# Turning tables by one DMA per tile in a one-core transformer block: the residual blocks join, one SwiGLU tile leaves

## The chip, the core and the metric

The kernel runs on one core of one Trainium2 chip. The metric is the device time of one execution in microseconds (us), as the median of several runs. Times of engines and of single instructions come from the hardware profiler's record of one execution. Engine names are those of the profile: PE is the matmul engine (PEld its weight loads), DVE the vector engine, ACT the scalar engine, POOL is GpSimd, and SP the engine whose queue starts nearly all transfers.

## The reference, cut to what matters

A block over 256 tokens (two tiles of 128) with a model width of 2048, in float32:

```python
h = rmsnorm(x, g_mix); proj = h @ w_in                     # two gated token mixers follow
x = x + (sigmoid(g_sb) * (y_sb @ w_sb_out) + sigmoid(g_ca) * (y_ca @ w_ca_out)) @ w_mix_out
h = rmsnorm(x, g_ffn)
g_ff, u_ff = split(h @ w_ffn_in, 2)                        # D_FF = 5632 each
x = x + (silu(g_ff) * u_ff) @ w_ffn_out
h = rmsnorm(x, g_ple)
x = x + sigmoid(h @ w_ple_gate) * (p @ w_ple_in)           # the "ple" gate, the last matrix
out = rmsnorm(x, g_final)
```

The weights are read from HBM once each and are most of the traffic (284 MB read in all).

## The kernel before

**Products.** Every matmul is split for float32 accuracy: the weights into a rounded part `hi` and a rest `lo` (ACT casts `hi`, DVE subtracts for `lo`), the activations likewise, and three products are added (hi·hi, hi·lo, lo·hi). The activations are the stationary operand. They lie transposed in *tables* (`T[:, kt, 0 or 1, token]`, part 0 the rounded one, part 1 the rest), where `kt` numbers the 128 rows of the inner dimension. Three tables matter here: `T3` (the residual for the FFN's input matmuls, 16 rows kt in 4 blocks of 512 columns of x), `T2` (the SwiGLU's result, one tile of 512 columns at a time), and `T1` (the residual for the last gate, "ple"). The names `T_5123`, `T_71` and `T_72` of the listings below are the places of T3, T1 and T2.

**Pieces.** The weights go by in *pieces* of two kt. A plain piece is 12 matmuls of 128x512. A *pair* piece takes two pieces' weights at once with sums and differences of them (a Strassen-like form, own accumulators `su`): 21 matmuls. Its weights pass through more casts: `L298` and `L301` for the two `hi`, `L304` for the sums (`T<-xf`). Pair pieces need sums of the table's blocks too, made by `sums_of` (tiles `fm`, then `FP`, `F_more` or `F_last`).

**Order.** A list `pieces` and the function `flush` set the order: for each piece it starts loads on SP's queue as one of seven places for raw weights comes free (`RAW` and `MORE` in this part of the program), splits up to three pieces ahead, issues the piece's products, and then runs whatever *asides* are due at that piece's number (`state["at"]`) and one of the waiting `tasks` (`later(fn)` puts a task back by three). Each engine works through its own instructions in the order in which the program issued them; semaphores join them. So an instruction that is issued early and waits holds everything behind it on its engine.

**The FFN** runs in three blocks of the hidden width, h0, h1 and h2, with 3, 4 and 4 SwiGLU tiles of 512 columns. Each block's input units are followed by out units that multiply the tiles with `w_ffn_out`. The FFN's first unit has no pair pieces: its 16 plain pieces (here p0 to p15) run through `T3` as it is, and in the meantime `scale_next` multiplies the table by the norm's factor (`L869`) and `pair_sums` makes the sums (`L890`, then `fm`), using the two work places called `af`.

**Two ways to turn a tile** stand in the kernel. `into_table` lets PE transpose 128x128 blocks into PSUM (8 per tile, `tp`), and `table_part` copies from there into the table: with a gain by ACT (`L556`) and DVE (`L557`). The residual blocks (four for `T3`, four for `T1`) and the mixers' gates go that way. `into_table_by_dma` splits the 32-bit words into 16-bit halves with two ACT copies (`L502`), transposes by two DMAs on SP's queue (`L505`, 128x8x128 each), and later joins the halves with two ACT copies for each half of the tile (`L513`), into a work place `af`, from which `table_part` fills the table (`L548` for a pair block). All 11 SwiGLU tiles go that way: the DMAs two pieces after the tile is made, the joins four and five pieces later.

Of the kernel before, what the change touches and what calls it, by code (L numbers as in the profile page):

```python
# [9 lines left out]
F32 = mybir.dt.float32  # L10
F32R = mybir.dt.float32r
U16 = mybir.dt.uint16
# [5 lines left out]
P = 128  # L18
S = 256
NT = 2  # L20
# [12 lines left out]
NB = 512  # L33
FB = 256
FF_BLOCKS = [12, 16, 16]

PAIRS = (2, 4, 6)
# [16 lines left out]
def block_kernel(ctx: ExitStack, tc: tile.TileContext, x, p, w_in, w_sb_out, w_ca_out, w_mix_out,  # L54
# [18 lines left out]
    nc = tc.nc  # L73
    dma_w = nc.sync
# [25 lines left out]
    x_ = bp.tile([P, NT, D], F32, tag="x", name="x")  # L100
# [52 lines left out]
    asides = []  # L153
    turning = set()
    done = set()
# [251 lines left out]
    state = dict(loaded=0, split=0, at=0, raw=0, hl=0, ext=0, ps=ps_mm, fourth=None, ring=0, places=0, hold=False)  # L407
    late = dict(ps=[ps_mm])
# [27 lines left out]
    def later(fn, n=3):  # L436

        for _ in range(n):
            tasks.append((None, lambda: None))
        tasks.append((None, fn))  # L440
# [53 lines left out]
        for k in range(4):  # L494
            done.add((key, 4 * c + k))

    def turn(src, planes, whole):

        words = src.bitcast(U16).rearrange("p t (n h) -> p t h n", h=2)
        planes = planes.bitcast(U16).rearrange("p t (h n) -> p t h n", h=2)  # L500
        for t in range(NT):
            nc.scalar.copy(planes[:, t], words[:, t])  # L502
        for t in range(NT):
            ts = slice(t * P, (t + 1) * P)
            dma_w.dma_start_transpose(whole[:, :, ts], planes[:, t].rearrange("p h n -> p (h n)"))  # L505

    def turned_part(dst, kt, turned, k0, gain, key, forms, pairs):

        af = state["work"]("af").rearrange("p (k s) -> p k s", k=2)
        words = af.bitcast(U16).rearrange("p k (s h) -> p h k s", h=2)  # L510
        with tc.issue_after(state["cast"].ins):
            for h in range(2):
                nc.scalar.copy(words[:, h], turned[h][:, k0 : k0 + 2, :])  # L513
        table_part(dst, kt + k0, af, gain, forms, pairs, af)
        for k in range(k0, k0 + 2):
            done.add((key, kt + k))

    def into_table_by_dma(dst, c, src, planes, rooms, key, gain=None, forms=None, pairs=PAIRS, wait=2):

        turned, whole = rooms  # L520
        turning.update((key, 4 * c + k) for k in range(4))
        at = state["at"] + wait
        steps = [(at, lambda: turn(src, planes, whole))]
        for i in range(2):
            steps.append((at + 4 + i, lambda i=i: turned_part(dst, 4 * c, turned, 2 * i, gain, key, forms, pairs)))
        asides.extend(steps)
        asides.sort(key=lambda v: v[0])

    def room_halves(v):

        v = v.rearrange("p t n -> p (t n)").bitcast(U16)
        return [u.rearrange("p (k s) -> p k s", s=S) for u in (v[:, :1024], v[:, 1024:])], v.rearrange("p (k s) -> p k s", s=S)

    def table_part(dst, kt, ps, gain, forms, pairs, af=None):
        n = ps.shape[1]
# [398 lines left out]
    room = bp.tile([P, 4096], F32R, tag="x", name="room")  # L934
# [81 lines left out]

    def next_tables(T, c, gain, key, pool):

        for cc in (c - 1, c):
            fn = lambda cc=cc: into_table(T, cc, x_[:, :, cc * NB : (cc + 1) * NB], gain, key, pool=pool)  # L1020
            if cc == c:
                tasks.append((None, fn))
            else:
                later(fn)
# [67 lines left out]
    def out_form(pairs):  # L1092
        return lambda kt: late["F"][1][pairs.index(kt // 2)]

    def hidden(dst, c, key, g, pairs):
        C = late["C"]
        into_table_by_dma(dst, c, C[:, :2, :], C[:, 2:, :], room_halves(C[:, :2, :]), key, forms=out_form(pairs), pairs=pairs)

    def in_post(dst, c, key, pairs):
        def post(g, b):  # L1100
# [37 lines left out]
    k0 = 0  # L1138
# [131 lines left out]
```

## Time and profile before

| | us |
|---|---|
| median of 3 runs | 1458.44 (1457.09 to 1458.54) |
| the profiled execution | 1458.38 |
| its span, first to last instruction | 1456.7 |
| PE busy in it | 1438.7 (99%) |
| DVE busy | 1248.6 (86%) |
| ACT busy | 869.8 (60%) |

The mean granted TensorE clock of that execution is 0.996 of full speed. Busy times are of one execution on the one core; a busy PE isn't a PE at its peak, since matmuls overlap each other by their pipeline. A row of a group reads: line, engine, operation, output and input with their sizes, count, then busy time, the mean of one in ns, and after the bar the idle time of the engine just before such instructions and what ended it. A row of the timeline reads: start, length, engine, line, operation, count, and in brackets the idle time before and what ended it.

### The profile page before, as it was taken

Reading aid. Unit: us, or ns where it says so; the run is one execution under the profiler, and the core shown is the slowest. Engines: PE = TensorE matmul, PEld = TensorE weight load, DVE = VectorE, ACT = ScalarE, POOL = GpSimd, SP = SyncE. Lnnn points to the kernel's source line nnn. Section 1 sums busy time; section 2 is a strip of 40 time slices with the busy share of each in tenths; the row PEclk is TensorE's granted clock in tenths of the full one; section 3 lists DMA queues with packets and bytes.
Section 4 is the critical chain, followed back from the end, with each engine's and each line's share of the span. In section 5 each row is a group of like instructions: output and inputs, shape, how many; then the busy total and the mean of one; then the engine's idle time right before and its main releaser. Section 6 shows DMA issues by size and latency. Waiting matters only on the chain.

```text
span 1456.7 us, 18609 instructions
## 1 busy us (share of the span) xinstructions
PE 1438.7 (99%) x6749; PEld 1200.4 (82%) x6749; DVE 1248.6 (86%) x1587; ACT 869.8 (60%) x1048; POOL 24.1 (2%) x44
## 2 busy tenths in 40 slices
PE   9999999999999999999999899999999999999997
PEld 7888888878888888888888688888888888887886
DVE  6879777888987767888989899999999999999775
ACT  6445555654545665555767555667755666776652
POOL 0200000000010000000000000000000000000000
PEclk9999999999999999999999999999999999999999
DMA  9866555566675556765675666776666766675771
GB/s 315 285 188 210 181 173 173 177 202 200 201 253 166 180 164 183 232 203 174 204 218 187 183 212 194 223 226 210 198 205 221 218 203 213 222 211 179 262 231 70
DMA packets 187964, 296.95 MB, mean 204 GB/s; under 512 B 32256, under 2 KB 65328, under 8 KB 187616
## 3 DMA queue, kind: packets, MB, share of 16 engines
q1 hardware_dynamic: 185760, 287.09, 63.6%
q0 software_dynamic: 2112, 8.68, 1.8%
q8 instruction: 53, 0.87, 0.3%
q14 instruction: 39, 0.32, 0.1%
HBM read 284.19 MB, written 5.77 MB: 199 GB/s over the span
## 4 chain that ended last, share of the span: by engine, by line
PE 89%; DVE 4%; DMA 3%; ACT 2%; issue 1%; SPq 0%; DVEq 0%; ACTq 0%
PE mm L313 63%; PE su L313 11%; PE mm L398 8%; PE mm L400 4%; DVE lo L260 2%; DMA C<-C 1%; DVE xf L260 1%; DMA raw<-in_w_ffn_out 1%; DMA raw<-in_w_ple_in 1%; PE tp L490 1%; ACT hi L283 1%; DMA raw<-in_w_ffn_in 0%; PE mml L313 0%; ACT af L513 0%; DVE raw L260 0%
## 5 line engine op out<-in xcount | busy, mean ns | idle before, releaser
L313 PE MATMUL mm<-hi,T 128*128 128x512 f32 x2650 | 855.1, 391 | 1.6 <-DVE v L902 1.0
L260 DVE TENSOR_TENSOR lo<-raw,hi 128x1024 fp32r<-128x1024 f32 (+1 forms) x517 | 624.4, 1217 | 114.0 <-ACT hi L283 100.8
L283 ACT CAST hi<-raw 128x1024 fp32r<-128x1024 f32 (+1 forms) x379 | 395.9, 1049 | 329.0 <-PE mm L313 205.8
L313 PEld LDWEIGHTS mm<-hi,T 128*128 128x128 f32 x2650 | 497.3, 188 | 106.4 <-issue 1.4
L313 PE MATMUL mm<-lo,T 128*128 128x512 f32 x1325 | 516.1, 390 | 0.0
L313 PEld LDWEIGHTS mm<-lo,T 128*128 128x128 f32 x1325 | 248.9, 188 | 51.0
L398 PE MATMUL mm<-T,hi 128*128 128x512 f32 x512 | 179.7, 398 | 0.0
L400 PE MATMUL mm<-T,lo 128*128 128x256 f32 x512 | 139.5, 280 | 0.0
L301 ACT CAST hi<-raw 128x1024 fp32r<-128x1024 f32 x69 | 72.6, 1052 | 77.3 <-DVE raw L260 28.0
L260 DVE TENSOR_TENSOR T<-xf,T 128x1536 fp32r<-128x1536 f32 x61 | 106.9, 1753 | 12.6 <-ACT T L304 12.5
L398 PEld LDWEIGHTS mm<-T,hi 128*128 128x128 f32 x512 | 94.5, 188 | 20.1
L260 DVE TENSOR_TENSOR xf<-raw 128x512 f32<-128x512 f32 x138 | 94.5, 685 | 13.8 <-DMA raw<-in_w_ffn_out 5.2
L304 ACT CAST T<-xf 128x1536 fp32r<-128x1536 f32 x61 | 90.3, 1480 | 20.3 <-DVE xf L260 19.7
L400 PEld LDWEIGHTS mm<-T,lo 128*128 128x128 f32 x512 | 96.5, 189 | 2.3
L298 ACT CAST hi<-raw 128x1024 fp32r<-128x1024 f32 x69 | 72.5, 1051 | 36.7 <-PE mm L313 21.8
L313 PE MATMUL mm<-T,T 128*128 128x512 f32 (+1 forms) x279 | 77.8, 373 | 0.0
L313 PE MATMUL su<-hi,T 128*128 128x512 f32 x170 | 66.3, 392 | 5.1 <-ACT T L548 5.1
L313 PEld LDWEIGHTS mm<-T,T 128*128 128x128 f32 x279 | 49.5, 189 | 9.2
L902 DVE TENSOR_TENSOR C<-su,C 128x512 f32<-128x512 f32 x72 | 47.6, 682 | 0.7 <-PE su L313 0.5
L260 DVE TENSOR_TENSOR xf<-raw,xf 128x512 f32<-128x512 f32 x69 | 47.2, 684 | 0.6
L260 DVE TENSOR_TENSOR raw<-raw 128x512 f32<-128x512 f32 x69 | 47.2, 684 | 0.3
L313 PE MATMUL su<-T,FP 128*128 128x512 f32 x174 | 47.2, 389 | 0.0
(280 smaller groups left out, 1266.0 us busy)
## 6 DMA issues: line engine op xcount, KB each, us to landing
raw<-in_w_ffn_in SPq DMA_DIRECT2D x176, 512.0 KB, 4.3
raw<-in_w_in SPq DMA_DIRECT2D x160, 512.0 KB, 4.3
raw<-in_w_ffn_out SPq DMA_DIRECT2D x88, 512.0 KB, 4.7
raw<-in_w_mix_out SPq DMA_DIRECT2D x32, 512.0 KB, 4.7
raw<-in_w_ple_gate SPq DMA_DIRECT2D x32, 512.0 KB, 5.1
raw<-in_w_sb_out SPq DMA_DIRECT2D x16, 512.0 KB, 3.8
raw<-in_w_ca_out SPq DMA_DIRECT2D x16, 512.0 KB, 4.5
x<-in_x SPq DMA_DIRECT2D x4, 512.0 KB, 10.6
```

Of the source, the lines that this page charges most:

```text
L260: return nc.vector.tensor_tensor(out, a, b, ALU.subtract)
L283: state["cast"] = nc.scalar.copy(hi[:, c : c + m], raw[:, c : c + m])
L298: nc.scalar.copy(h1, raw1)
L301: nc.scalar.copy(h2, raw2)
L304: nc.scalar.copy(xh, xf)
L313: state["mm"] = nc.tensor.matmul(ps, u, v, start=first, stop=last, skip_group_check=True)
L398: nc.tensor.matmul(ps, hi[:, i, f], lhs[:, kt, :, :].rearrange("p c s -> p (c s)"), start=a, stop=False)
L400: nc.tensor.matmul(ps[:, :S], lo[:, i, f], lhs[:, kt, 0, :], start=False, stop=z)
L490: nc.tensor.transpose(ps[:, k, t * P : (t + 1) * P], src[:, t, (k0 + k) * P : (k0 + k + 1) * P], ident)
L902: nc.vector.tensor_tensor(C[i], q, C[j], ALU.add)
```

## The change

- `by_dma` takes the place of `turn`, `turned_part`, `into_table_by_dma` and `room_halves`. It issues one DMA transpose of 128x16x128 per tile, not two of 128x8x128, and one join copy of 128x2x512 for each half of a tile, not two of 128x512. The caller gives the piece numbers of the DMA and of the first join.
- The last SwiGLU tile of h0 (`c == 2`) goes back to PE: 8 transposes through `later(into_table)`.
- `next_tables`: the four residual blocks for `T3` and the first two for `T1` ("ple") go by DMA. The first block of a unit is split into `C[:, :2]` and turned into an own place `turned` (DMA one piece later, joins five and six later); the second is split into `C[:, 2:]` and turned into `C[:, :2]`, that is into the place which the first DMA reads (three, seven and eight pieces later). The ple blocks 2 and 3 stay on PE.

So PE transposes of tables and gates go from 96 to 56 (8 for the h0 tile are new, 48 for six residual blocks are gone), and DMA transposes from 22 small to 16 large ones.

```diff
-    def turn(src, planes, whole):
...
-    def turned_part(dst, kt, turned, k0, gain, key, forms, pairs):
...
-    def into_table_by_dma(dst, c, src, planes, rooms, key, gain=None, forms=None, pairs=PAIRS, wait=2):
...
+    def by_dma(dst, c, src, planes, turned, key, at, gain=None, forms=None, pairs=PAIRS):
+
+        words = src.bitcast(U16).rearrange("p t (k n h) -> p t h k n", h=2, n=P)
+        planes, turned = (v.rearrange("p t n -> p (t n)").bitcast(U16) for v in (planes, turned))
+        split = planes.rearrange("p (h k t n) -> p t h k n", h=2, k=4, t=NT)
+        halves = turned.rearrange("p (h k s) -> p h k s", h=2, k=4)
+
+        def turn():
+            for t in range(NT):
+                nc.scalar.copy(split[:, t], words[:, t])
+            dma_w.dma_start_transpose(turned.rearrange("p (j s) -> p j s", s=P), planes)
+
+        def join(k0):
+            af = state["work"]("af").rearrange("p (k s) -> p k s", k=2)
+            with tc.issue_after(state["cast"].ins):
+                nc.scalar.copy(af.bitcast(U16).rearrange("p k (s h) -> p h k s", h=2), halves[:, :, k0 : k0 + 2, :])
+            table_part(dst, 4 * c + k0, af, gain, forms, pairs, af)
+            for k in range(k0, k0 + 2):
+                done.add((key, 4 * c + k))
+
         turning.update((key, 4 * c + k) for k in range(4))
+        asides.extend([(state["at"] + at[0], turn), *((state["at"] + at[1] + i, lambda i=i: join(2 * i)) for i in range(2))])
         asides.sort(key=lambda v: v[0])
...
     def next_tables(T, c, gain, key, pool):
+        C = late["C"]
+        room = late["pool"].tile([P, 2, NB], F32, tag="turned", name="turned")
         for cc in (c - 1, c):
+            if key == "ffn" or cc < 2:
+                planes, turned, at = (C[:, :2, :], room, (1, 5)) if cc < c else (C[:, 2:, :], C[:, :2, :], (3, 7))
+                by_dma(T, cc, x_[:, :, cc * NB : (cc + 1) * NB], planes, turned, key, at, gain)
+                continue
...
     def hidden(dst, c, key, g, pairs):
         C = late["C"]
-        into_table_by_dma(dst, c, C[:, :2, :], C[:, 2:, :], room_halves(C[:, :2, :]), key, forms=out_form(pairs), pairs=pairs)
+        if key == "h0" and c == FF_BLOCKS[0] // 4 - 1:
+            later(lambda: into_table(dst, c, C[:, :2, :], key=key, pool=g["pool"], forms=out_form(pairs), pairs=pairs))
+        else:
+            by_dma(dst, c, C[:, :2, :], C[:, 2:, :], C[:, :2, :], key, (2, 6), forms=out_form(pairs), pairs=pairs)
```

What this does to the order of work is seen on two engines and one queue. In the changed kernel the lines below `by_dma` have other numbers: `L506` is the split copy (`L502` before), `L507` the DMA (`L505`), `L512` the join (`L513`), `L543` and `L544` the table's parts with a gain (`L556`, `L557`), `L856` the scaling of the table (`L869`), `L877` the pair sums' copy (`L890`).

**ACT in the FFN's first unit,** in the engine's order (an `xN` sums up equal neighbours), from the norm's sums (`jk,sum_ffn`) to the pair sums' first cast (`FP<-fm`). Before:

```order
L283 CAST hi<-raw 128x1024
L125 ACTIVATE jk,sum_ffn<-x 128x512 x2
L283 CAST hi<-raw 128x1024 x2
L556 ACTIVATE T_5123<-tp,gT 128x256 x4
L283 CAST hi<-raw 128x1024
L556 ACTIVATE T_5123<-tp,gT 128x256 x4
L283 CAST hi<-raw 128x1024 x6
L478 CAST FP<-fm 128x512
L283 CAST hi<-raw 128x1024 x3
```

With the change, from the table's block 2 (kt 8 to 11) to the second `FP`:

```order
L543 ACTIVATE T_5123<-af,gT 128x256 x2
L283 CAST hi<-raw 128x1024
L543 ACTIVATE T_5123<-af,gT 128x256 x2
L283 CAST hi<-raw 128x1024 x6
L478 CAST FP<-fm 128x512
L512 COPY af<-C 128x2x512
L283 CAST hi<-raw 128x1024
L543 ACTIVATE T_5123<-af,gT 128x256 x2
L512 COPY af<-C 128x2x512
L543 ACTIVATE T_5123<-af,gT 128x256 x2
L304 CAST T_71<-xf 128x1536
L478 CAST FP<-fm 128x512
```

Before, both blocks' parts (two times four `L556`) stood ahead of the six casts and of `FP`. With the change block 3 (kt 12 to 15) is joined only behind the first `FP`, and its first `L543` stands behind one cast more, that of p15, which waits for p11's matmuls, since it takes the place of p11's `hi`.

**ACT in the last out unit of h2,** where ple blocks 0 and 1 are turned. Its second half runs plain and pair pieces in the order 0,0,1,-2,1,-4,3,-5,3,-6,7,7 (a minus is a pair piece). Before, from the sums of pair -2 (`L304`) to `L301` of pair -5:

```order
L304 CAST T_5123<-xf 128x1536
L556 ACTIVATE T_71<-tp,gT 128x256
L125 ACTIVATE jk,sum_ple<-x 128x512 x2
L556 ACTIVATE T_71<-tp,gT 128x256
L298 CAST hi<-raw 128x1024
L556 ACTIVATE T_71<-tp,gT 128x256 x4
L283 CAST hi<-raw 128x1024
L556 ACTIVATE T_71<-tp,gT 128x256 x2
L301 CAST hi<-raw 128x1024
L298 CAST hi<-raw 128x1024
L304 CAST T_5123<-xf 128x1536
L283 CAST hi<-raw 128x1024
```

With the change, from the joins of block 0 to that same `L301` of pair -5, the last row:

```order
L512 COPY af<-turned 128x2x512 x2
L301 CAST hi<-raw 128x1024
L304 CAST T_5123<-xf 128x1536
L298 CAST hi<-raw 128x1024
L543 ACTIVATE T_71<-af,gT 128x256 x4
L283 CAST hi<-raw 128x1024
L512 COPY af<-C 128x2x512
L543 ACTIVATE T_71<-af,gT 128x256 x2
L512 COPY af<-C 128x2x512
L543 ACTIVATE T_71<-af,gT 128x256 x2
L301 CAST hi<-raw 128x1024
```

The eight table parts stood ahead of pair -4's `L301` before. Between `L304` of pair -4 and `L301` of pair -5 there was one cast; now there are two casts, two joins and all eight table parts.

**SP's queue** (transfers, summed up where they repeat). Before, around the FFN's start and at h0's last tile:

```order
L244 DMA raw<-in_w_mix_out 128x2x512 x32
L244 DMA raw<-in_w_ffn_in 128x2x512 x26
L505 DMA_TRANSPOSE C<-C 128x8x128 x2
L244 DMA raw<-in_w_ffn_in 128x2x512 x19
L505 DMA_TRANSPOSE C<-C 128x8x128 x2
L244 DMA raw<-in_w_ffn_in 128x2x512 x3
L244 DMA raw<-in_w_ffn_out 128x2x512 x14
L505 DMA_TRANSPOSE C<-C 128x8x128 x2
```

With the change:

```order
L244 DMA raw<-in_w_mix_out 128x2x512 x27
L507 DMA_TRANSPOSE turned<-C 128x16x128
L244 DMA raw<-in_w_mix_out 128x2x512 x2
L507 DMA_TRANSPOSE C<-C 128x16x128
L244 DMA raw<-in_w_mix_out 128x2x512 x3
L244 DMA raw<-in_w_ffn_in 128x2x512 x11
L507 DMA_TRANSPOSE turned<-C 128x16x128
L244 DMA raw<-in_w_ffn_in 128x2x512 x2
L507 DMA_TRANSPOSE C<-C 128x16x128
```

Four transposes now stand among the loads for the mixers' last matrix and the FFN's first; the second of each two waits for the first one's landing, with the loads behind it. The pair for h0's last tile is gone.

More of the change, by code (lines that the diff above doesn't have):

```diff
@@ L495, in into_table @@
             done.add((key, 4 * c + k))
-    def turn(src, planes, whole):
[L499 to L505, printed above, removed]
-    def turned_part(dst, kt, turned, k0, gain, key, forms, pairs):
[L509 to L516, printed above, removed]
@@ L518, in into_table_by_dma @@
-    def into_table_by_dma(dst, c, src, planes, rooms, key, gain=None, forms=None, pairs=PAIRS, wait=2):
-        turned, whole = rooms
-        turning.update((key, 4 * c + k) for k in range(4))
[L522 to L526, printed above, removed]
+    def by_dma(dst, c, src, planes, turned, key, at, gain=None, forms=None, pairs=PAIRS):
[14 more added lines that the diff above has]
+                done.add((key, 4 * c + k))
+        turning.update((key, 4 * c + k) for k in range(4))
+        asides.extend([(state["at"] + at[0], turn), *((state["at"] + at[1] + i, lambda i=i: join(2 * i)) for i in range(2))])
@@ L527, in into_table_by_dma @@
         asides.sort(key=lambda v: v[0])
-    def room_halves(v):
-        v = v.rearrange("p t n -> p (t n)").bitcast(U16)
-        return [u.rearrange("p (k s) -> p k s", s=S) for u in (v[:, :1024], v[:, 1024:])], v.rearrange("p (k s) -> p k s", s=S)
     def table_part(dst, kt, ps, gain, forms, pairs, af=None):
```

## Prediction

> **What bounds the kernel now.** I read the page's busy times first, then its chain and PE's waits, and then the timeline around the longest wait.
>
> ```profile
> PE 1438.7 (99%) x6749; PEld 1200.4 (82%) x6749; DVE 1248.6 (86%) x1587; ACT 869.8 (60%) x1048; POOL 24.1 (2%) x44
> PE 89%; DVE 4%; DMA 3%; ACT 2%; issue 1%; SPq 0%; DVEq 0%; ACTq 0%
> PE su L313 <- ACT T L548: 5.1, 1, 5.1
> PE warm L628 <- POOL mhalf L109: 1.2, 1, 1.2
> ```
>
> PE sets the time: 99% busy and 89% of the chain. So only three things count: matmul work taken from or given to PE, stalls of PE, and its clock. Of its waits one stands out, 5.1 us in a single place; the next is 1.2. The profiled execution (1458.38) agrees with the median of the runs (1458.44), so the sum can stand on either.
>
> The long wait belongs to h0's last tile. First the chain that ends there, then PE and SP, then PE in three windows (length, busy with count, granted clock, DMA share, GB/s):
>
> ```profile
> 801.35 0.81 SPq L505
> 802.22 7.47 DMA C<-C
> 809.77 1.38 ACT af L513 x2
> 812.39 0.62 ACT T L548
> ...
> 806.23 0.62 PE L313 MATMUL mm<-hi,T 128*128 128x512 f32 x2
> ...
> 806.91 0.62 PE L313 MATMUL mm<-hi,T 128*128 128x512 f32 x2
> ...
> 807.59 0.39 PE L313 MATMUL mm<-hi,T 128*128 128x512 f32 x1
> 813.05 0.79 PE L313 MATMUL su<-hi,T 128*128 128x512 f32 x1 [5.08 <-ACT T L548]
> 800.80 5.51 SPq L505 DMA_TRANSPOSE C<-C  x2
> 797.00:807.50 10.50, 10.50 (x48) 1.00 0.94 178
> 813.00:819.00 6.00, 5.95 (x14) 0.50 0.50 165
> 819.00:830.00 11.00, 11.00 (x49) 1.00 0.33 98
> ```
>
> Two DMA transposes take 7.47 us to land while the 16 DMA engines are 94% taken; then come the joins (`L513`), the table (`L548`), and only then a matmul. And the six microseconds that follow run at half clock.
>
> **The change part by part.** *h0's tile back to PE: the stall.* Three matmuls take 806.91 − 806.23 = 0.68, a pitch of 0.2267 each, so a plain piece of twelve is 2.72. From 807.59 to 813.05 are 5.46 us, so 5.2 are lost. With PE's own transposes there is no transfer and no join. −5.2. What comes next behind it is the copy of the transposes out of PSUM, some tenths; the later pieces' casts were done by 805.79 + 1.05 already, so nothing else is waiting there.
>
> *The clock after it.* 14 matmuls took 6.0 us; at the full pitch they take 3.2. −2.8, as long as no new stall is long enough to do the same.
>
> *PE transposes.* The residual blocks' transposes, as they stand among matmuls (timeline), with their group and the table parts that go with them:
>
> ```profile
> 669.53 0.40 PE L313 MATMUL mm<-hi,T 128*128 128x512 f32 x1
> 669.76 1.04 PE L490 MATMUL tp<-ident,x 128*128 128x128 f32 x8
> 670.56 0.48 PE L313 MATMUL mm<-hi,T 128*128 128x512 f32 x1
> L490 PE MATMUL tp<-ident,x 128*128 128x128 f32 x64 | 8.5, 272 | 0.0
> L556 ACT ACTIVATE T<-tp,gT 128x256 fp32r<-128x256 f32 x32 | 13.6, 473 | 3.5 <-DVE T L557 3.0 <-PE tp L490 0.5
> ```
>
> From 669.76 to 670.56 eight transposes hold PE for 0.80 us, and in none of the 64 did PE wait (idle 0.0). Six tiles gone: −4.8. One tile (h0's) back: +0.8. The Trainium skill's page "VectorE: DVE Perf Modes", section "Rules for kernel authors", speaks against this part: a 128x128 transpose should go to TensorE where PSUM is acceptable as its destination, and to the DMA's crossbar otherwise. By it the six tiles would bring nothing and only h0's return would gain: −5.2 − 2.8 + 0.8 = −7.2, or 1451.2. The rows above show PE as the engine in short supply, and the sum below has the six near break-even, so rule and sum come out close together here for different reasons.
>
> *What the DMA way costs elsewhere.* Rows of the lines that split, transpose and join:
>
> ```profile
> L502 ACT COPY C<-C 128x1024 uint16<-128x1024 uint16 x22 | 22.2, 1041 | 1.2 <-DVE C L1107 1.0 <-DVE C L1087 0.2
> L513 ACT COPY af<-C 128x512 uint16<-128x512 uint16 x44 | 30.6, 768 | 11.9 <-DMA C<-C 11.5 <-DVE T L260 0.4
> L505 SPq DMA_TRANSPOSE C<-C x22: 1242/1291/4087, 709.7 to 1286.4; - x22
> DMA to landing us min/median/max: 2.7/3.1/8.1
> ```
>
> Per tile ACT pays two copies of 1.04 and two joins. The new join (128x2x512) isn't in the trace: as a plain copy of 1024 elements it would be 1.04, as two of the old ones 2 x 0.77 = 1.54; I take 1.3, since its strides are the old ones but one start is saved. That is 4.7 us a tile, 28 for six, on an engine with 40% idle: it costs only where a PE-needed cast queues behind it. For the ten SwiGLU tiles that stay, two starts each are saved; PE waited for none of them in the trace (the waits list has the one at h0 alone), so 0. The large transpose moves twice the data of one small one: between 3.1 (as one) and 8.1 us (the worst). I take 5, from the pair of small ones that together take two issues of 1.29 and a landing of 3.1.
>
> Whether a cast queues is a question of the order, at two places.
>
> *Place B, the FFN's first unit.* What ran there before:
>
> ```profile
> 672.19 1.90 DVE L557 SCALAR_TENSOR_TENSOR T<-tp,gT,T 128x256 fp32r<-128x256 f32 x4
> 676.12 0.60 PE L140 MATMUL rps<-dg,ones 128*128 128x256 f32 x2
> 676.76 0.43 DVE L141 COPY p2bc<-rps 128x256 f32<-128x256 f32 x1 [0.81 <-PE rps L140]
> 677.22 1.89 DVE L869 TENSOR_TENSOR T<-T,p2bc 128x512 fp32r<-128x512 f32 x3
> 679.03 1.22 DVE L260 TENSOR_TENSOR lo<-raw,hi 128x1024 fp32r<-128x1024 f32 x1
> 686.05 0.28 DVE L474 TENSOR_TENSOR fm<-af 128x128 f32<-128x128 f32 x1
> 689.31 0.63 ACT L478 CAST FP<-fm 128x512 fp32r<-128x512 f32 x1 [0.60 <-DVE fm L260]
> 658.00:702.00 44.00, 44.00 (x204) 36.59 (x203) 38.47 (x64) 23.42 (x33) 0.72 (x1) 1.00 0.61 178
> ```
>
> Before, the table's last block was complete at 672.19 + 1.90 = 674.1, far ahead of its use by p12. With the change its first join needs an `af` place that the pair sums still hold, and stands behind their `FP` on ACT. I work it through in time from the unit's start. The norm's `rps` follows 69 matmuls in the new order (15.6 us at 0.2267), and `p2bc` starts 0.64 behind it as in the rows: 16.3. From there to the end of `fm`, each instruction counted to the next one's start (0.08 before its end, as 677.22 + 1.89 stands to 679.03), DVE has in its new order one `p2bc` (0.4), six `lo` (1.14 from one start to the next), ten scalings (0.60), one sums' copy (0.60), two table parts (0.45, from 1.90 for four) and four `fm` (0.20): 15.5 us, and it ends at 31.8. `FP` 0.6, join 1.3, p15's cast 0.95, first table part 0.45: p12 can start at 35.1. PE has done p0 to p11 at 12 x 2.72 + 0.25 = 32.9. Stall: 2.2 us. It can't be under 1.4, since p15's cast waits for p11's end and the table part stands behind it; with a join of 1.54 and DVE waits of a few tenths it is 3. I take 2.2. DVE then has the rest of block 3, the pair sums and a pair piece's sums ahead of the `lo` of the next unit's first piece, 11.8 us of work from p15's cast on against four pieces (10.9) of PE: 0.5 more, between 0 and 1.5. B: +2.7 (1.4 to 4.5).
>
> *Place C, the last out unit of h2.* Before, around pairs -2, -4 and -5:
>
> ```profile
> 1328.98 0.83 ACT L556 ACTIVATE T<-tp,gT 128x256 fp32r<-128x256 f32 x2
> 1338.21 1.20 PE L313 MATMUL su<-T,T 128*128 128x512 f32 x4 [0.34 <-DVE T L260]
> 1342.57 1.47 ACT L304 CAST T<-xf 128x1536 fp32r<-128x1536 f32 x1
> 1348.84 1.06 ACT L301 CAST hi<-raw 128x1024 fp32r<-128x1024 f32 x1 [1.27 <-DVE raw L260]
> 1350.29 0.40 PE L313 MATMUL su<-hi,F_last 128*128 128x512 f32 x1
> 1350.89 0.49 PE L313 MATMUL mm<-hi,T 128*128 128x512 f32 x1 [0.21 <-ACT hi L283]
> 1313.00:1355.00 42.00, 41.39 (x185) 32.51 (x184) 40.01 (x49) 28.71 (x38) 0.58 (x1) 1.00 0.59 191
> ```
>
> From the end of pair -4's sums (1342.57 + 1.47 = 1344.0) ACT now has two casts (2 x 0.95), two joins (2.6) and eight table parts (8 x 0.41, by 0.83 for two): 7.8, so `L301` of pair -5 starts at 1351.8 and its `hi` is there at 1352.8, where PE wanted it at 1350.3: a stall of 2.5. Against that, the eight DVE parts leave the stretch ahead of pair -2, and two small waits of before go: about 0.6 at 1338.21 and 0.3 at 1350.89. C: +1.6, between 0 (if ACT runs ahead by the idle time it has in this window, 42 − 28.7) and 4 (DVE has 40 of 42 us busy, so PE can hardly use the 1.6 us of transposes that it is freed of here, on top of the stall).
>
> The joins in the second mix unit (table blocks 0 and 1) come some ten pieces ahead of their use, by p0 to p7; their cover is that distance. 0, and up to 1 if it is gone.
>
> *SP's queue.* Each of the six new transposes stands among weight loads, and the second of each two waits for the first's landing: a hold of 5 + 4 (the longest issue, 4087 ns) = 9 us. Seven raw places at 2.72 us a piece, less some 4.5 us of landing, leave 14.5 us. 0 here; the price beyond it is a rival.
>
> Sum: −5.2 − 2.8 − 4.8 + 0.8 + 2.7 + 1.6 = −7.7, from 1458.4: 1450.7 us. Bounds: with B and C at their low ends −10.6, at their high ends and 1 for the mix unit −2.5, that is 1447.8 and 1455.9.
>
> **The rivals.** *All of it is hidden:* the joins find ACT idle and no stall is new: −12.0, 1446.4. For it: ACT 60% busy. Against: the order itself puts p15's cast ahead of the table part that p12 waits for.
>
> *The six blocks cost more than they free.* The new stalls come to 8 to 12 us: B and C at their high ends are 8.5, the mix unit's pair pieces wait for joins too, or a stall grows to a length that halves the clock and costs 2.8 more. Then −12.0 + 8 to 12 gives 1454.4 to 1458.4, and from 1455.5 on nothing is seen, since 0.2% or 2.9 us is about what this measurement can tell from no change. For it: DVE's share in both places (38.5 of 44, 40 of 42), so that whatever comes late can't be made up. Against: the same DVE work stood there before, a little earlier, and a delay in one place isn't passed to the other, 600 us away.
>
> *Slower: SP's queue held too long.* At the second transpose of a pair SP waits for the first's landing with all weight loads behind it. If a large transpose lands as late as two worst small ones (2 x 8.1), the hold is 16.2 + 4.1 = 20.3, 5.8 over the 14.5 of the places, and a stall of that length halves the clock as at 813: 5.8 + 2.8 = 8.6 at such a place. One place brings 1459.3 and two bring 1467.9; the gain is gone from a hold of about 19.4 on. For it: the landing of 7.47 at 802, when the DMA share was 0.94. Against: the share is 0.61 and 0.59 in the windows of B and C, and the median landing 3.1.
>
> *The clock.* The rows say that a PE stall of 5.2 us cost 2.8 more at half clock, while the waits of 1.2 and less left the mean clock of the page at 0.996. Whether 2.2 to 2.5 us do so isn't in the trace; if both did, the time would be 1450.7 + 5.6 = 1456.3. I take the nearer row in length, the 1.2, and price it at 0. The Trainium skill's page "TensorE: Matmul & The Clock Gate", section "What's actually happening", puts the drop after an idle window of about 3.4 us and the return after a busy one as long: by it the stall at h0 would have cost an estimated 1.7 (half of one window), where the trace shows 2.8, and stalls of 2.2 to 2.5 would cost nothing.
>
> **How the numbers follow.** My forecast's mechanism, small stalls at B and C within their bounds, 1447.8 to 1454.4: 0.58. All hidden, 1445.5 to 1447.8: 0.12. Faster than that, 0.03. The six blocks cost more than they free, or the clock drops in one or both places, 1454.4 to 1459: 0.19, of which 0.05 lies below 1455.5. SP held, above 1459: 0.08. So faster by over 0.2% (below 1455.5) has 0.58 + 0.12 + 0.03 + 0.05 = 0.78; of the rest 0.14 within 0.2% and 0.08 slower. The range 1446.4 to 1457.5 leaves out about 2 in 10.
>
> **What would show it.** Right: no wait of PE for the table at h0's last tile, no window at clock 0.50 there, PE matmuls 40 fewer, PE busy about 7 lower (the clock's 2.8 and 4.0 of transposes). Place B: PE waits about 2 us for ACT's table part (`L543`) in the FFN's first unit. Place C: PE waits for `hi` of pair -5 (`L301`). Wrong: a wait for loads or transposes on SP's path, a new window at 0.50, or joins that wait for their DMA with casts behind them.

## The result, and the profile after

| | before | after |
|---|---|---|
| median, us | 1457.67 (7 runs, 1455.83 to 1458.54) | 1452.93 (7 runs, 1450.80 to 1454.66) |
| ratio | | 0.9966 [0.9956, 0.9976] |
| span of the profiled execution, us | 1456.7 | 1451.2 |

The change makes the kernel 5.0 us faster (3.5 to 6.4, the ratio on 1457.67). The forecast was 7.7 us, so the direction and the range held and a third of the forecast gain is missing. The page of the changed kernel, and PE's waits in it (line numbers are now those of the changed kernel):

```profile
PE 1434.7 (99%) x6709; PEld 1195.6 (82%) x6709; DVE 1248.7 (86%) x1587; ACT 889.1 (61%) x1047; POOL 23.2 (2%) x44
PE 93%; DVE 3%; ACT 2%; issue 1%; DMA 1%; SPq 0%; DVEq 0%; ACTq 0%
PE mm L313 <- ACT T L543: 2.1, 1, 2.1
PE mm L313 <- ACT hi L301: 1.5, 1, 1.5
PE warm L615 <- POOL mhalf L109: 1.2, 1, 1.2
```

The 5.1 us at h0's last tile are gone, with 40 matmuls fewer. Two waits have come that were not there: `L543` is the table part in the FFN's first unit (place B of the prediction), `L301` a pair piece's cast in h2's last out unit (place C). The timeline at B, ACT and then PE:

```profile
686.35 1.05 ACT L283 CAST hi<-raw 128x1024 fp32r<-128x1024 f32 x1 [1.66 <-PE mm L313]
687.46 0.62 ACT L478 CAST FP<-fm 128x512 fp32r<-128x512 f32 x1
687.98 1.34 ACT L512 COPY af<-C 128x1024 uint16<-128x1024 uint16 x1
689.19 1.03 ACT L283 CAST hi<-raw 128x1024 fp32r<-128x1024 f32 x1
690.13 0.90 ACT L543 ACTIVATE T<-af,gT 128x256 fp32r<-128x256 f32 x2
...
688.20 0.39 PE L313 MATMUL mm<-hi,T 128*128 128x512 f32 x1
690.69 0.50 PE L313 MATMUL mm<-hi,T 128*128 128x512 f32 x1 [2.10 <-ACT T L543]
```

Here one sees the queue that the order of work foretold: `FP`, the join, p15's cast and only then the table part that PE waits for. At C, the same two engines:

```profile
1326.51 1.71 ACT L543 ACTIVATE T<-af,gT 128x256 fp32r<-128x256 f32 x4
1328.12 1.03 ACT L283 CAST hi<-raw 128x1024 fp32r<-128x1024 f32 x1
1329.40 1.36 ACT L512 COPY af<-C 128x1024 uint16<-128x1024 uint16 x1 [0.25 <-DVE T L544]
1330.80 0.91 ACT L543 ACTIVATE T<-af,gT 128x256 fp32r<-128x256 f32 x2
1331.62 1.34 ACT L512 COPY af<-C 128x1024 uint16<-128x1024 uint16 x1
1332.99 0.91 ACT L543 ACTIVATE T<-af,gT 128x256 fp32r<-128x256 f32 x2
1333.80 1.03 ACT L301 CAST hi<-raw 128x1024 fp32r<-128x1024 f32 x1
...
1334.88 0.50 PE L313 MATMUL mm<-hi,F_more 128*128 128x512 f32 x1 [1.50 <-ACT hi L301]
```

And the windows of PE behind both (length, busy with count, granted clock, DMA share, GB/s):

```profile
691.00:694.40 3.40, 3.40 (x10) 0.51 0.76 251
694.40:700.00 5.60, 5.60 (x26) 0.99 0.10 33
1335.50:1339.40 3.90, 3.69 (x10) 0.59 0.63 201
1339.40:1345.00 5.60, 5.60 (x26) 0.98 0.33 95
```

Both new waits are followed by a stretch at half clock, though the longer of them is 2.1 us (2.3 over one pitch).

To see where time went, I add up for each kernel and stage by how much the starts of successive product matmuls (`L313`) lie more than the pitch of 0.2267 us apart. That counts waits and slow clock alike; PE's table transposes (0.1 us each) are counted apart. The windows' ends lie in stretches without losses. All in us, from one profile of each kernel; the names are those of the experiments below:

| kernel | transposes | FFN start, 650-720 | h0's end, 760-860 | h1's end, 1000-1060 | h2's end, 1250-1310 | last out unit, 1310-1357 | all from 590 us on |
|---|---|---|---|---|---|---|---|
| before | 96 | 0.4 | 8.1 | 0.0 | 0.0 | 2.5 | 12.3 |
| after | 56 | 4.2 | 0.2 | 0.0 | 0.0 | 6.3 | 11.8 |
| e1_h0_only | 104 | 0.4 | 1.3 | 1.8 | 3.1 | 1.7 | 9.7 |
| e5_small_dmas | 104 | 0.4 | 2.2 | 0.0 | 0.1 | 3.1 | 7.0 |
| e2_ffn4 | 72 | 3.5 | 0.2 | 0.2 | 1.2 | 1.4 | 7.7 |
| e3_ple2 | 88 | 0.4 | 1.3 | 2.4 | 2.9 | 5.4 | 14.5 |
| e10_h0_halves | 104 | 0.4 | 1.4 | 1.8 | 2.5 | 1.8 | 9.3 |
| e7_join6 | 72 | 0.2 | 6.7 | 1.3 | 0.4 | 1.4 | 11.3 |
| e9_halves | 72 | 1.9 | 3.0 | 0.6 | 1.5 | 1.4 | 9.7 |
| e8_ple_late | 56 | 1.4 | 3.5 | 0.1 | 0.8 | 4.3 | 11.3 |
| e14_loads_behind | 104 | 0.4 | 1.3 | 0.0 | 1.2 | 3.4 | 8.1 |
| e15_ffn4_loads_behind | 72 | 3.8 | 0.3 | 0.0 | 0.2 | 2.9 | 8.3 |
| e16_h0_dma | 48 | 4.0 | 5.3 | 0.0 | 0.7 | 5.9 | 17.2 |

From before to after: h0's end −7.9, transposes −4.0, the FFN's start +3.8, the last out unit +3.8, the rest −0.2: −4.5 of the 5.5 us by which the two spans differ. The other 1.0 us lies ahead of 590 us, where the order of work is the same in both; that part's losses went from 4.1 to 5.7 us over these profiles, and nothing is read from it.

### The profile page after: what moved, and what is told of

Read it like the earlier page. It is cut to its first block, busy times and chain, and to the rows that moved or that the text cites. A ratio compares the mean times of both kernels' runs of the same rounds, so it can differ in the third digit from the quotient of the medians.

```text
span 1451.2 us, 18508 instructions
## 1 busy us (share of the span) xinstructions
PE 1434.7 (99%) x6709; PEld 1195.6 (82%) x6709; DVE 1248.7 (86%) x1587; ACT 889.1 (61%) x1047; POOL 23.2 (2%) x44
## 4 chain that ended last, share of the span: by engine, by line
PE 93%; DVE 3%; ACT 2%; issue 1%; DMA 1%; SPq 0%; DVEq 0%; ACTq 0%
PE mm L313 66%; PE su L313 12%; PE mm L398 8%; PE mm L400 4%; DVE lo L260 1%; DMA raw<-in_w_in 1%; DMA raw<-in_w_ple_in 1%; ACT hi L283 1%; PE tp L490 0%; ACT af L512 0%; PE mml L313 0%; DVE xf L260 0%; PE xps L571 0%; ACT C L506 0%; DVE raw L260 0%
## 5 line engine op out<-in xcount | busy, mean ns | idle before, releaser
L313 PE MATMUL mm<-hi,T 128*128 128x512 f32 x2650 | 855.9, 391 | 3.3 <-ACT T L543 2.1
L313 PEld LDWEIGHTS mm<-hi,T 128*128 128x128 f32 x2650 | 498.1, 188 | 109.0 <-ACT T L543 2.5
L313 PE MATMUL mm<-lo,T 128*128 128x512 f32 x1325 | 517.3, 391 | 0.7 <-DVE lo L260 0.7
L313 PEld LDWEIGHTS mm<-lo,T 128*128 128x128 f32 x1325 | 249.3, 188 | 53.1 <-DVE lo L260 1.7
L301 ACT CAST hi<-raw 128x1024 fp32r<-128x1024 f32 x69 | 72.6, 1052 | 73.2 <-DVE raw L260 32.6
L304 ACT CAST T<-xf 128x1536 fp32r<-128x1536 f32 x61 | 90.2, 1479 | 26.1 <-DVE xf L260 26.0
L313 PE MATMUL mm<-T,T 128*128 128x512 f32 (+1 forms) x279 | 77.5, 371 | 0.0
L313 PE MATMUL su<-hi,T 128*128 128x512 f32 x170 | 65.7, 391 | 0.2 <-ACT hi L298 0.2
L313 PEld LDWEIGHTS mm<-T,T 128*128 128x128 f32 x279 | 49.2, 188 | 9.1
L313 PE MATMUL su<-T,FP 128*128 128x512 f32 x174 | 47.9, 389 | 0.0
```

Of the source, the lines that this page charges most:

```text
L301: nc.scalar.copy(h2, raw2)
L304: nc.scalar.copy(xh, xf)
L313: state["mm"] = nc.tensor.matmul(ps, u, v, start=first, stop=last, skip_group_check=True)
```

## The experiments

All are timed against the kernel before. The theory going in: the gain is that of h0's tile and of the transposes, and what is missing was given back at B and C by ACT's queue and by the clock. The rival: h0's return brings less than its stall.

**The parts, one at a time.** e1 leaves only h0's return and the single large DMA of the other ten tiles; e5 is the kernel before with h0's return alone; e2 and e3 are e1 with the four ffn or the two ple blocks on the DMA way.

```diff
 # e1, e2, e3: next_tables of the changed kernel
-            if key == "ffn" or cc < 2:
+            if False:                       # e1
+            if key == "ffn":                # e2
+            if key != "ffn" and cc < 2:     # e3
 # e5: hidden of the kernel before
+        if key == "h0" and c == FF_BLOCKS[0] // 4 - 1:
+            later(lambda: into_table(dst, c, C[:, :2, :], key=key, pool=g["pool"], forms=out_form(pairs), pairs=pairs))
+        else:
             into_table_by_dma(...)
```

> The changed kernel with all residual blocks turned by PE again: only h0's last tile (PE instead of DMA) and the single large DMA for the other ten tiles are left of the change. Theory 'stalls and clock' (the profile after: the six blocks cost a stall of 2.3 us and a half-clock stretch of 1.8 us in the FFN's first unit, and 4.2 us net in h2's last out unit, against 4.8 us of PE transposes that they free): h0's return alone is worth 5.2 + 2.8 - 0.8 = 7.2 us, ratio to the kernel before about 0.995, some 2 to 3.5 us faster than the changed kernel; no PE wait over 1.3 us in the FFN. Rival 'the tile returned to PE brings less than its stall, and the six blocks bring their 4.8 us': about the time of before, -0.2 us.

> The kernel before with one edit: h0's last tile goes back to PE; the other ten tiles keep two small DMAs and four join copies. Theory: the single large DMA and the single join copy are off PE's path, so this is the same as the run with the large DMAs and h0 on PE, within 0.5 us, -7.2 us against before. Rival 'the large DMA itself gains or costs on PE's path': the two differ by more than 1 us; the FFN's out units (PE waits behind joins) would show where.

> The changed kernel with the two ple blocks back on PE; the four ffn blocks stay on the DMA way. Theory 'stalls and clock': -7.2 - 3.2 + 4.1 = -6.3 us against before, the PE wait for L543 of about 2.1 us in the FFN's first unit and a clock of 0.5 for some 3.4 us behind it are still there, nothing new around 1320 to 1345 us. Rival 'six blocks bring 4.8': -3.4 us.

> The changed kernel with the four ffn blocks back on PE; the two ple blocks stay on the DMA way. Theory 'stalls and clock': -7.2 - 1.6 + 4.2 = -4.6 us against before, the waits around L301 of pair -5 and a half-clock stretch of some 3.5 us behind them are still there, and no stall in the FFN's first unit. Rival 'six blocks bring 4.8': -1.8 us.

| | median, us | ratio to before |
|---|---|---|
| e1_h0_only | 1455.45 | 0.9989 [0.9979, 0.9999] |
| e5_small_dmas | 1453.44 | 0.9969 [0.9957, 0.9980] |
| e2_ffn4 | 1451.79 | 0.9954 [0.9941, 0.9966] |
| e3_ple2 | 1459.88 | 1.0012 [1.0003, 1.0021] |

e2's time came as expected (−6.7 by its ratio against −6.3), its mechanism only in part: the wait for `L543` is there, but no half clock behind it. e1, e3 and e5 did not come: h0's return alone brings 1.6 us with large DMAs and 4.5 with small ones, not 7.2. At h0's end itself e1 and e3 gain 6.8 us of the changed kernel's 7.9, and e5 gains 5.9 (what is left there in e5 are waits of 0.5 us and less). What e1 and e3 give back stands at the ends of h1 and h2, which lose 4.9 and 5.3 us that before, e5 and the changed kernel don't lose. There the joins wait for their DMA. SP, ACT and PE at h2's end in e1:

```profile
1282.45 1.50 SPq L244 DMA_DIRECT2D raw<-in_w_ffn_out  x2
1284.01 5.98 SPq L507 DMA_TRANSPOSE C<-C  x1
1292.13 1.35 ACT L512 COPY af<-C 128x1024 uint16<-128x1024 uint16 x1 [3.78 <-DMA C<-C]
...
1294.86 0.73 PE L313 MATMUL su<-T,T 128*128 128x512 f32 x2 [1.30 <-ACT T L304]
```

The join starts 8.1 us behind the issue, and `L304`, which PE waits for, behind the join.

**Is it the size of the DMA?** e10 is e1 with each of those tiles issued as two DMAs of 8 blocks.

```diff
-            dma_w.dma_start_transpose(turned.rearrange("p (j s) -> p j s", s=P), planes)
+            for q in range(2 if dst is T2 else 1):
+                n = 2048 if dst is not T2 else 1024
+                dma_w.dma_start_transpose(turned[:, q * n : q * n + n].rearrange("p (j s) -> p j s", s=P), planes[:, q * n : q * n + n])
```

> The run with all residual blocks on PE and h0's last tile on PE, with one edit: each of the ten tiles' transposes is issued as two DMAs of 8 blocks instead of one of 16; copies and joins as there. That run lost 1.8 and 3.0 us of PE time at the ends of h1 and h2 (joins that waited 6 to 9 us from the DMA's issue), where the kernel with the old small DMAs and h0 on PE lost 0 and 0.1. Theory 'one large transpose lands late at the block ends': the joins there wait 4 to 5.5 us from the issue, the loss is under 0.5 us in both places, and the time falls by some 3 to 4 us, to about 0.9965 of before. Rival 'the size does not matter, the losses there come from the moment at which the tile is made': same time as that run (0.999 of before, within 1 us), and the losses at the two block ends stay over 1 us.

1456.00 us, 0.9992 [0.9983, 1.0001]; the losses at the two ends are 1.8 and 2.5 us. My theory fell and the rival held: the size makes no difference that these runs could tell. What differs is what stands ahead on SP's queue. In e5 the transposes at h1's end are issued 0.9 us behind one weight load, with the next one 5.1 us ahead, and the join follows 5.5 us after the first issue; in e1 two loads were issued 1.0 and 2.2 us ahead, and it takes 8.5.

**Loads behind the transpose.** e14 is e1, and e15 is e2, with the next load that the program issues after a SwiGLU tile's transpose ordered behind it.

```diff
+            state["turn"] = dma if dst is T2 else None      # dma: the transpose, in turn()
...
+            with ExitStack() as order:
+                if state.get("turn") is not None:
+                    order.enter_context(tc.issue_after(state.pop("turn").ins))
                 state["load"] = dma_w.dma_start(dst, src)
```

> The run with only h0's last tile on PE (all residual blocks on PE), with one edit: the next weight load that the program issues after a SwiGLU tile's transpose is ordered behind it on SP's queue, so that at the ends of h1 and h2 ten or eleven loads of w_ffn_out stand ahead of the transpose, not fourteen. In the traces so far the transposes there land 5.0 to 6.3 us after their issue when one load was issued in the 1.5 us ahead of them, and 6.1 to 9.1 when there were two in 2.3 us, whatever their size. Theory 'a transpose waits behind the weight loads issued just ahead of it': the landing falls to 4 to 5.5 us, the losses at the two block ends (1.8 and 3.0 us) to under 0.5, the time by 3 to 4.5 us to about 0.9965 of before. Rival 'loads behind it slow it as much (the DMA engines are full either way)': landings stay at 7 us or more and the time at 0.999. Either way, if the held loads come late, PE waits for DMA of raw appear.

> The run with the four ffn blocks on the DMA way and ple on PE (0.9954), with the same edit for the SwiGLU tiles. Theory: its losses at the ends of h1 and h2, 0.2 and 1.2 us, go, the wait in the FFN's first unit (3.5 us) stays: some 1.4 us less, about 0.9945 of before. Rival 'the order of loads matters elsewhere as well': the scheduler gives the time back in the out units, and it is no better than 0.9954.

e14: 1452.71 us, 0.9966 [0.9953, 0.9978], against 0.9989 for e1. Its h2 end, SP and ACT:

```profile
1273.79 0.37 SPq L247 DMA_DIRECT2D raw<-in_w_ffn_out  x1
1280.53 1.63 SPq L510 DMA_TRANSPOSE C<-C  x1
1282.21 2.27 SPq L247 DMA_DIRECT2D raw<-in_w_ffn_out  x4
...
1284.20 1.37 ACT L516 COPY af<-C 128x1024 uint16<-128x1024 uint16 x1 [0.60 <-DMA C<-C]
```

With 6.7 us between the last load and the transpose, the join starts 3.7 us behind the issue, although four loads follow at once; the losses at both ends are 0.0 and 0.1 (the other 1.1 us of its 1250-1310 stand at 1307.8, where PE waits for a `lo` at the start of the next unit). So the loads issued just ahead make a transpose late, and those behind it do not.

The issue and landing times of all large transposes, in nine traces that have only such (e6 left out), put it more exactly. For 108 of them a weight load was issued less than 2.35 us ahead; they landed 1.75 to 3.9 us after the last of these loads had landed, half of them within 2.03 us. Nine had no load in the 6 us ahead, and they landed 3.65 to 3.69 us after their own issue. So it is the landing of the loads ahead that counts, more than their number. e15 gained nothing by the same edit: 0.9959 [0.9946, 0.9971] against e2's 0.9954. Its two ends are nearly free of losses too (0.0 and 0.2 where e2 lost 0.2 and 1.2), and the last out unit loses 2.9 us where e2's lost 1.4: given back, as the rival said.

**h0's tile in the company of the rest.** e16 is the changed kernel with that tile on DMA again (`if False:` in `hidden`).

> The changed kernel with its one PE part undone: h0's last tile goes by DMA again, all six residual blocks stay on the DMA way. Theory of the prediction: the stall and the half clock at h0's end come back, 5.2 + 2.8 less 0.8 = 7.2 us slower than the changed kernel, about 1.0015 of before. Rival 'the stall there was a matter of the loads ahead of it': with one load in the 2 us ahead of the transpose it lands in 5 to 6 us, the stall is 2 us at most with no half clock, and the kernel is within 2.5 us of the changed one, 0.998 or less.

1456.97 us, 0.9993 [0.9983, 1.0004]: 3.9 us slower than the changed kernel by the ratios, between the two expectations. One load stands 0.9 us ahead of the transpose there and the next 5.0; before, two stood 0.4 and 1.6 us ahead. The landing is 6.4 us after the issue, where before it was 8.9 after the first of the two, and PE's wait is half as long:

```profile
799.24 0.37 SPq L244 DMA_DIRECT2D raw<-in_w_ffn_out  x1
800.13 3.47 SPq L507 DMA_TRANSPOSE C<-C  x1
806.99 0.39 PE L313 MATMUL mm<-hi,T 128*128 128x512 f32 x1
809.79 0.50 PE L313 MATMUL su<-hi,T 128*128 128x512 f32 x1 [2.42 <-ACT T L535]
```

So the stall of 5.2 us was not the price of a DMA transpose as such, but of one behind two loads: those landed 5.6 us after the transposes' first issue before, and the one in e16 3.6 after.

**Places B and C.** e7 is e2 with the second ffn block's joins one piece earlier; e9 is e7 with two DMAs of 8 blocks for the SwiGLU tiles; e8 is the changed kernel with the joins of e7 and with the ple joins four pieces later.

```diff
-... (C[:, :2, :], room, (1, 5)) if cc < c else (C[:, 2:, :], C[:, :2, :], (3, 7))
+... (C[:, :2, :], room, (1, 5)) if cc < c else (C[:, 2:, :], C[:, :2, :], (3, 6 if key == "ffn" else 7))   # e7, e9
+... (C[:, :2, :], room, (1, 5 if key == "ffn" else 9)) if cc < c else (C[:, 2:, :], C[:, :2, :], (3, 6 if key == "ffn" else 11))   # e8
```

> The run with the four ffn blocks on the DMA way and ple on PE, with one edit: the second ffn block's joins are due six and seven pieces after its unit, not seven and eight, so that block 3's first join stands ahead of the pair sums' first cast FP on ACT. Theory 'the first join behind FP and p15's cast makes p12 wait': the loss of 3.5 us in the FFN's first unit falls to 0.4, and the time by some 3 us against that run, to about 0.993 of before. Rival 'DVE has no room there, the wait only moves': the loss in 650 to 720 us stays over 2 us and the time at 0.9954.

> The run with the earlier join of block 3, and besides it the ten SwiGLU tiles' transposes as two DMAs of 8 blocks each (the four ffn blocks keep one large DMA). Theory 'one large transpose lands late at the block ends': the losses at the ends of h1 and h2 (1.4 us together with large DMAs and the ffn blocks on DMA) go to under 0.5, and the time by about 1 us below the run with the earlier join alone, to about 0.992 of before. Rival 'the size does not matter': no difference between the two.

> The changed kernel with block 3's earlier join and with the ple blocks' joins due nine to twelve pieces after their unit instead of five to eight, so that ACT does not have two joins and eight table parts ahead of L301 of pair -5. Theory 'ACT's queue ahead of L301 of pair -5 makes the stall': the loss between 1310 and 1357 us falls from 6.3 us to about 2.5 (before: 2.5), no half-clock stretch there, and with block 3's 3.8 the time falls some 7 us against the changed kernel, to about 0.992 of before. Rival 'DVE is full in this stretch (40 of 42 us), whatever the order on ACT': the loss there stays over 4.5 us.

| | median, us | ratio to before |
|---|---|---|
| e7_join6 | 1451.18 | 0.9967 [0.9955, 0.9978] |
| e9_halves | 1452.23 | 0.9969 [0.9957, 0.9980] |
| e8_ple_late | 1452.40 | 0.9970 [0.9959, 0.9981] |

At B the mechanism is shown: with the first join of block 3 ahead of `FP`, the wait for the table is gone and the FFN's start loses 0.2 us in e7, not 3.5.

```profile
672.03 1.35 ACT L512 COPY af<-C 128x1024 uint16<-128x1024 uint16 x1
673.25 1.03 ACT L283 CAST hi<-raw 128x1024 fp32r<-128x1024 f32 x1
674.19 0.91 ACT L543 ACTIVATE T<-af,gT 128x256 fp32r<-128x256 f32 x2
...
689.29 0.62 ACT L478 CAST FP<-fm 128x512 fp32r<-128x512 f32 x1
```

The time, though, did not fall: e7 loses 6.7 us at h0's end where e2 lost 0.2. Its order of work differs from e2's up to there, since the kernel's scheduler sorts each engine's instructions anew, and near 785 us PE now waits for a cast and for a copy of the residual into PSUM (`L354`), with a half-clock stretch behind them:

```profile
784.18 0.49 PE L313 MATMUL mm<-hi,T 128*128 128x512 f32 x1 [1.13 <-ACT hi L283]
786.38 0.79 PE L313 MATMUL mm<-hi,T 128*128 128x512 f32 x1 [1.71 <-ACT mm L354]
```

e9 has the same kind of loss (3.0), and its two block ends lose 2.1 us together against e7's 1.7: the size of the DMAs makes no difference here either. In e8 the last out unit loses 4.3 us, not 2.5 as my theory had it and not quite the over 4.5 of the rival; the wait at pair -5 is gone and others stand at pair -6 and behind it. DVE is busy for 43.59 of the 47 us of that window in e8, 42.07 in the changed kernel. That it is DVE's load that keeps 4 us there is likely and not shown.

**The clock.** e6 is e1 with fifteen weight casts repeated 7 to 14 times each (the same result, more work for ACT), so that PE waits at many places.

> A probe of the clock: the run with only h0's last tile on PE, where fifteen casts of weights are repeated 7 to 14 times each (same result), so that ACT makes PE wait at fifteen or more places for about 0.5 to 8 us. In the traces so far a PE wait of 5.2 us, one of 2.3 us, and two of 1.3 and 2.0 us within 2 us of each other were followed by 2.9, 1.8 and 1.4 us of half-clock loss, and one of 2.2 us by none. Theory 'a window that runs free of the program decides': waits under 1.5 us never halve the clock, waits of over about 3.4 us always do, and between them some do; the loss of each is near 1.7 us or a multiple, up to about 3.4. Rival 'a fixed length decides': one threshold parts them.

One execution, 1638.66 us, clock 0.950. The traces' record of the granted clock says more than the lengths of the waits. In all fourteen traces each stretch at half clock between the first microseconds and the kernel's end is 3.41 us long or a multiple of it (up to 17.07 in e6), and the changes of one trace lie whole multiples of 3.413 us apart: in the changed kernel the clock drops at 691.05 and at 1336.17, 189 of them later. So time is cut into windows of 3.41 us whose ends don't follow the program (where a trace has no other change, I count them back from the drop at the kernel's end). PE in such windows (length, busy with count, granted clock, DMA share, GB/s), three of the changed kernel and three of e15:

```profile
687.64:691.05 3.41, 1.31 (x7) 1.00 0.85 243
691.05:694.47 3.42, 3.42 (x10) 0.50 0.76 252
694.47:697.88 3.41, 3.41 (x17) 1.00 0.13 46
...
685.53:688.94 3.41, 2.75 (x13) 1.00 0.77 246
688.94:692.35 3.41, 1.87 (x8) 1.00 0.77 281
692.35:695.77 3.42, 3.42 (x17) 1.00 0.59 168
```

The changed kernel's wait at B falls whole into one window, and the next window runs at half clock. The same wait in e15, 0.1 us longer, is cut in two by the end of a window, and the clock stays. I count PE's idle time in every window, with each matmul as one pitch (the rows show a matmul as 0.39 us long). Of 5795 windows at full clock, the first and last 20 us of each trace left out, 23 were followed by half clock. These had 2.09 us of idle time or more, all the others 2.08 or less. Half clock then lasted until the end of the first window in which PE idled less than about 0.9 us.

The waits by length (over one pitch), the idle time of the window behind which the clock dropped (or else the idlest one there), the stretch at half clock, and the loss, 0.2 us for each matmul begun in it:

| waits, us | at | idle in the window, us | half clock behind, us | loss, us |
|---|---|---|---|---|
| 5.2 | before, 807.6 | 3.41 | 6.83 | 2.8 |
| 2.6 | e16, 807.0 | 2.24 | 3.41 | 1.4 |
| 2.4 | e15, 687.9 | 1.70 | none | none |
| 2.3 | after, 688.2 | 2.37 | 3.41 | 1.6 |
| 2.2 | e2, 689.2 | 1.37 | none | none |
| 2.1 | e16, 688.2 | 2.24 | 3.41 | 1.6 |
| 1.3 and 2.0 | e7, 782.7 | 3.19 | 3.41 | 1.6 |
| 1.7, smaller ones around it | after, 1333.0 | 2.28 | 3.41 | 1.6 |
| 1.7, smaller ones around it | e16, 1338.1 | 2.09 | 3.41 | 1.4 |
| 1.7, smaller ones around it | e3, 1341.1 | 1.66 | none | none |
| 0.9 | e6, 871.2 | 0.62 | none | none |
| 1.4 and 1.8, 4 us apart | e6, 396.0 | 1.36 | none | none |
| 5.2 and 12.2 | e6, 1437.4 | 3.41 | 17.07 | 1.8 |
| 4.4 and 10.3 | e6, 1071.5 | 3.19 | 13.65 | 1.6 |
| 3.4, 3.6 and 1.8 | e6, 781.5 | 3.19 | 10.24 | 2.8 |

The theory holds and the rival falls: no length of a single wait parts the cases, the idle time within one window does. Waits of 3.4 us and more were always followed by half clock; of those from 1.7 to 2.6 us it was the place in the window, and what else PE waited for in it, that decided. One thing came otherwise than expected: the loss is no multiple of 1.7 us and doesn't grow with the wait, since most of a long stretch passes while PE still waits (1.8 us behind twelve microseconds). e6 has sixteen such stretches, with 1.2 to 4.2 us lost in each; three of them stand in the table.

## Why the prediction was right, and where it was not

*h0's tile and its clock, −5.2 − 2.8.* Right: 8.1 us of losses went to 0.2. e16 puts a smaller price on it in the changed kernel's company, 3.9 us: the prediction took the landing of 7.47 us as the tile's own, and it was that of a transpose behind two loads.

*Transposes, −4.0 net.* Right: PE has 40 matmuls fewer at 0.1 us. That PE's busy time also fell by 4.0 does not show it: the prediction's sign was some 7 (4.0 and the clock's 2.8), and what the clock gave at h0's end went again at B and C.

*B, +2.7.* The wait was foretold as 2.2 and is 2.1 by the profile, with its cause and its order on ACT; e7 shows the cause. The 0.5 of DVE's backlog behind it did not come in the changed kernel and in e16, where a half-clock stretch stands behind the wait; in e2 and e15, which have none, 0.9 and 1.0 us came at 703 and 702. That the half clock gives DVE the time to catch up fits these four and is not shown otherwise.

*C, +1.6.* The queue on ACT ahead of `L301` of pair -5 is there. The working matched it with the wrong rows of before: `F_last` and the cast at 1348.84 belong to pair -6, and pair -5 is `F_more`, with its cast at 1340.65. The queue was right, and the price came out near by luck: without the half clock the losses there grew by 2.2 us (6.25 − 1.6 − 2.47). With the rows of pair -5 the same sum gives 1334.88 + 1.48 + 7.8 + 1.0 = 1345.2 for the `hi`, which PE wanted at 1342.2: a stall of 3.0, or 2.1 net of the 0.9.

*The clock behind B and C, 0.* This is the term that was mis-sized. From the windows above the two stretches cost 3.40 x 0.49 = 1.7 and 3.90 x 0.41 = 1.6 us, together 3.3, where the sum said 0 since it took the 1.2 us wait as the nearer row. That is the difference between −7.7 and the −4.5 of the table; the misses at B and C, 0.6 over and 0.6 under, cancel each other. The step that failed is the choice of the 1.2 us wait as a measure: what counts is the idle time in one window of 3.41 us, 2.09 and more here, and the window of each of the two places had 2.37 and 2.28. Whether such a wait pays is thus a matter of where it falls, and B's paid nothing in e2 and e15. Two further things are luck for the number. The clock's drop had been put with the rival, above 1454.4, at 2.8 for each place; it came in both, and the time still fell into the band of the forecast's mechanism because each cost 1.6 or 1.7. And the 3.3 is that of the profiled execution: one such stretch takes 0.0012 off the mean clock, and the kernel's end 0.0013 or more in these traces, so the two timed executions at 0.998 had at most one, and they were hardly faster (1452.42 and 1452.53 against 1452.93). How much of the 3.3 would come back as other waits is open. By the rule on the clock gate that the prediction quotes from the Trainium skill's page "TensorE: Matmul & The Clock Gate", section "What's actually happening", such waits were to cost nothing. The traces do not agree that a whole window must be idle, with drops behind 2.09 us of idle time and more in 3.41.

*The prediction's signs.* Those on the waits came: none for the table at h0's end, one for `L543` at B, one for `L301` at C. One of its signs of being wrong came too, the new windows at 0.50.

*The ten tiles that stay, 0, and SP's queue, 0.* Right for this kernel (0.0 at the ends of h1 and h2). That it wasn't safe is shown by e1, e3 and e10, where the same tiles there lost 4.3 to 5.3 us. The two loads ahead stand in the changed kernel too (1.2 and 2.3 us, 1.0 and 2.1): its landings of 6.1 and 6.7 us were just early enough. e1's were 8.5 and 8.1. At h2's end the loads explain it: they landed 4.7 us behind the transpose's issue in the changed kernel and 6.2 in e1, and the transpose 1.9 us later in both. At h1's end they explain 0.9 of the 2.4 us; the rest stays open.

*The rivals.* "All hidden" fell at B and C. "The six blocks cost more than they free" is half right: by the losses, the four ffn blocks freed 3.2 us and cost 3.8, the two ple blocks freed 1.6 and cost 3.8, while e1, without them, is slower all the same. "SP held too long" did not come: no PE wait for a load appeared.

## What to carry to other kernels

Moving work off the bounding engine is paid for in the queue that takes it: read, in the order of work, what stands ahead of the instruction for which the bounding engine waits, and price the wait with the clock that may halve behind it. A DMA transpose that is waited for wants no bulk load issued in the 2 us ahead of it, since here it landed some 2 us after such loads; ordering the loads behind it brought 3 us in one kernel (e14 against e1) and nothing in another (e15 against e2). Where a scheduler sorts the instructions, an edit can move small waits elsewhere by as much as it gains (e7, e9, e15), so parts measured alone need not add up; of the kernels here e2, with the ffn blocks by DMA and the ple blocks on PE, has the lowest ratio, 0.9954 [0.9941, 0.9966], which is not parted from the changed kernel's 0.9966.

## What the runs showed of the hardware that was not expected

- The granted TensorE clock changed only at the ends of windows of 3.413 us that don't follow the program. Of 5795 windows at full clock in fourteen traces, those with 2.09 us or more of PE idle time (23) were followed by half clock and those with 2.08 or less were not, so the wait at B, 2.1 to 2.4 us long, cost 1.6 us of clock in two kernels (after and e16) and none in two others (e2 and e15). The loss did not grow with the wait: 1.4 to 2.8 us outside e6, and 1.8 behind waits of 5.2 and 12.2 us in it.
- A DMA transpose's landing depended on the loads issued just ahead. At the ends of the FFN's blocks it took 3.7 us with none in the last 6 us, 5.0 to 6.4 with one and 6.1 to 9.1 with two in the last 2.3 us; elsewhere in the blocks one load gave 3.7 to 7.1. Behind a load issued less than 2.35 us ahead it landed 1.75 to 3.9 us after that load, in half of 108 cases within 2.03. One transpose of 16 blocks or two of 8 made no difference (8.1 against 8.0 us to the join at h2's end of e1 and e10).
